# Attention of one block of queries for both kv heads at once, on the two halves of the array; the sums of squares of the mixer's outputs added on DVE

## The chip, the cores and the metric

The kernel runs on one NeuronCore of a Trainium2 chip, as one program. The metric is the device time of one execution in microseconds (us). Five engines run their own instruction streams and wait for each other through semaphores: TensorE (PE, the 128x128 matmul array, with its weight loads shown as PEld), VectorE (DVE), ScalarE (ACT), GpSimd (POOL) and SyncE (SP), which issues the DMAs.

## The reference, cut to what matters

One layer of a hybrid decoder is computed for 1024 prompt positions and 32 sample positions: a half-step FFN, a mixer, a second half-step FFN and a final norm. In the mixer one projection gives q, k, v, u and g. Half of the mixer's output is sliding-window attention, the other half a gated product (gMLP); each half is normalised by itself before the output projection.

```python
def _sink_attention(q, k, v, dist, valid, sinks):
    s = einsum('...qhgd,...khd->...hgqk', q, k) / sqrt(HEAD_DIM)
    s = s - slopes[:, :, None, None] * dist
    s = where(valid, s, -inf)
    p = softmax(concatenate([s, sink], axis=-1), axis=-1)[..., :-1]
    return einsum('...hgqk,...khd->...qhgd', p, v)

def _merge(attn, gate, attn_out_norm, gmlp_out_norm, w_out):
    return concatenate([rmsnorm(attn, attn_out_norm), rmsnorm(gate, gmlp_out_norm)], -1) @ w_out
```

There are 2 kv heads of 64 channels, and 4 query heads go with each (8 query heads in all). The 1024 prompt positions form 8 blocks of 128 queries; a block sees its own 128 keys and the 128 before it (the first block only its own).

## The kernel before

Activations lie with channels on the 128 partitions and tokens along the free axis. Tokens are cut into two halves `h` of 528 (512 of the prompt and 16 of the samples). q, k and v are kept in f32: `QT[h]` has four tiles g of 128 partitions, kv head 0 on partitions 0-63 and kv head 1 on 64-127; `KT` holds the keys in the same way, and `VT` the values with keys on the partitions and the two heads' channels side by side in 128 columns.

The mixer is a list of jobs. For each half come 14 projections (k, v, q0-3, u0-3, g0-3; PSUM tiles `pp`) and then, behind those of both halves, the output projections (`pw`; first the gate's four jobs, then attention's four, for each half). A unit of a projection is 24 matmuls (three for each of eight slices of the contraction, since every f32 operand is split into a high and a low part), a unit of an output projection 12. The weights of a job are loaded into one of six `raw` buffers, cast to a high part on ACT (`whi`, line 114), and the rest is subtracted on DVE or POOL (`wlo`, line 115).

Everything else in the mixer is written as generators that are run in between. The class `Interleave` keeps a clock of PE time, and after each unit it lets as many pieces run as a rate and a credit allow. A piece yields two numbers: the PE time that it cost, and how long its results take, from the table `LAT`; its next piece is run once the clock has passed that. Of the pending generators at most `I.width` run at a time: 1 in the first half's projections, 2 afterwards. After these rules Tile, the layer below, still moves instructions by its own priorities, sets the waits, and gives out buffers. [...]

`attention(b, c)` (lines 844 to 890) treats block b for kv head c, four query heads at a time. First piece: scores `sc` (line 862), two heads to a PSUM bank, on the 64 partitions of head c; a DVE instruction (line 866) that adds the position bias and takes the maximum; `nm`, the negated maximum (867); exp on ACT with the sum (869); the sink's share (870 to 873); and P times the reciprocal (875). Second piece: P is transposed on PE (`ptr`, 881) and copied to `PT` by ACT (882). Third piece: P V into `po` (886), with all 128 columns of `VT` as weights, so that both heads' channels come out, of which ACT copies the 64 partitions of head c over q (888). `count(h, 0, 9)` counts eight such generators and the samples' attention of a half; with the ninth, `norm_out` is put in the queue.

`norm_out(h, which)` takes the squares of the outputs on ACT and adds them (`squares`, line 176, into `oacc`), on POOL unless another engine is given; PE then sums over partitions (`pn`, 150), DVE takes the reciprocal root in some twelve small instructions (`tiny_rsqrt`, 136 to 141), and PE spreads it (`pr`, 165). `spatial` (the gate) transposes g on PE into a PSUM bank `pt` (788), normalises it into `gn` (816, 819) and multiplies it by the spatial weights (`pm`, 835; `mix`, 839). `out_proj` evaluates a unit on DVE (`wo`, 981) and adds it to x on POOL (983). There are eight PSUM banks in the mixer's pool; every `pst` takes one.

Of the kernel before, what the change touches and what calls it, by code (L numbers as in the profile page):

```python
# [11 lines left out]
F32 = mybir.dt.float32  # L12
# [3 lines left out]
AF = mybir.ActivationFunctionType  # L16
ALU = mybir.AluOpType
# [15 lines left out]
RATE = [0.5, 0.67, 0.7, 0.5]  # L33
ON_POOL = {0: (), 1: (), 2: (1, 4, 6)}
STEPS = [(1, 5, 0, 2), (1, 0, 1, 1), (1, 1, 1, 1)]
LAT = {"rstd": 9.0, "gate": 14.7, "qk": 8.5, "pt": 2.5, "gelu": 7.2, "squares": 7.6, "sample": 12, "burst": 6.5, "keys": 9.6, "norm": 6.5, "factors": 10}
GELU_A = 0.044715 ** 0.5
GELU_C = 0.7978845608028654

# [1 line left out]
def build(nc, tc, ctx, A):  # L41
    dbl = ctx.enter_context(tc.tile_pool(name="dbl", bufs=30))
    gp = ctx.enter_context(tc.tile_pool(name="g", bufs=4))
    wp = ctx.enter_context(tc.tile_pool(name="w", bufs=8))
# [13 lines left out]
    V, S, G, PE = nc.vector, nc.scalar, nc.gpsimd, nc.tensor  # L58
# [6 lines left out]
    def gtile(nm, shape=(128, 2, H)):  # L65
        return gp.tile(list(shape), F32, tag="g", name=nm)
# [4 lines left out]
    def pst(nm):  # L71
        return ps.tile([128, 512], F32, tag="ps", name=nm)
# [9 lines left out]
    def small(nm, n=4, p=128):  # L82
        return sp.tile([p, n], F32, tag=f"s_{nm}", name=nm, bufs=1 if nm[0] == "s" else 2 if nm[0] == "g" else 3)
# [13 lines left out]
    ident = cp.tile([128, 128], F32, name="ident")  # L97
# [622 lines left out]
    I = Interleave()  # L720
    finished, have_v = {}, set()

    def count(h, which, of):

        finished[h, which] = finished.get((h, which), 0) + 1
        if finished[h, which] == of:
            finished[h, which] = True
            I.later(norm_out(h, which), wait=LAT["norm"])

# [111 lines left out]
        V.scalar_tensor_tensor(u, m[:, :n], 0.5, u, op0=ALU.mult, op1=ALU.mult)  # L841


    def attention(b, c):
        h, o = b // 4, 128 * (b % 4)
        assert h in have_v
        nk = 256 if b else 128
        rows = slice(64 * c, 64 * c + 64)
        ks = T0[h] + o - 128 if b else 0
        keys = KT[rows, ks:ks + nk]  # L850
        if b == 4:
            keys = KT[rows, 384:672].rearrange("p (a k) -> p a k", a=2)[:, :, :128]
        Pt = gtile("P", (128, 4, 256))
        mx, nm, sm = small("mx"), small("nm"), small("den")
        for j in range(2):
            s = pst("sc")
            for i in range(2):
                g = 2 * j + i
                out = s[:, i * 256:i * 256 + nk]
                if b == 4:  # L860
                    out = out.rearrange("p (a k) -> p a k", a=2)
                PE.matmul(out, lhsT=QT[h](g, o, 128)[rows], rhs=keys, start=True, stop=True)
            for i in range(2):
                g = 2 * j + i
                hd = 4 * c + g
                V.tensor_tensor_reduce(Pt[:, g, :nk], s[:, i * 256:i * 256 + nk], alibi[:, hd, 256 - nk:], 1.0, sinks[:, hd:hd + 1], ALU.add, ALU.max, mx[:, g:g + 1])  # L866
        V.tensor_scalar_mul(nm, mx, -1.0)
        for g in range(4):
            S.activation(Pt[:, g, :nk], Pt[:, g, :nk], AF.Exp, bias=nm[:, g:g + 1], accum_out=sm[:, g:g + 1])
        V.tensor_add(mx, nm, sinks[:, 4 * c:4 * c + 4])  # L870
        S.activation(mx, mx, AF.Exp)
        V.tensor_add(sm, sm, mx)
        V.reciprocal(sm, sm)
        for g in range(4):
            V.tensor_scalar_mul(Pt[:, g, :nk], Pt[:, g, :nk], sm[:, g:g + 1])
        yield 1.8, LAT["qk"]
        PT = gtile("PT", (128, 2, 512))
        for kc in range(nk // 128):
            pt = pst("ptr")
            for g in range(4):  # L880
                PE.transpose(pt[:, g * 128:(g + 1) * 128], Pt[:, g, kc * 128:(kc + 1) * 128], ident)
            S.copy(PT[:, kc, :], pt)
        yield 0.9, LAT["pt"]
        po = pst("po")
        for kc in range(nk // 128):
            PE.matmul(po, lhsT=VT[:, max(b - 1, 0) + kc, :], rhs=PT[:, kc, :], start=(kc == 0), stop=(kc == nk // 128 - 1))  # L886
        for t in range(2):
            S.copy(QT[h].t[t][rows, :, o:o + 128], po[rows, t * 256:(t + 1) * 256].rearrange("p (g q) -> p g q", g=2))
        count(h, 0, 9)
        yield 1.7, 1  # L890


    def sample_attention(h):
        ck = tmp("ck")[:, :512].rearrange("p (b k) -> p b k", b=4)
        load(ck, A["ckT"][:, 4 * h:4 * h + 4, :])
        bc = tmp("bc")[:, :144]
        load(bc, A["sb"])
        bd = tmp("bd")[:, :128].rearrange("p (b r) -> p b r", b=4)
        G.memset(bd, 0.0)
        for c in range(2):  # L900
            rows = slice(64 * c, 64 * c + 64)
            for g in range(4):
                G.tensor_copy(bd[rows, :, 16 * c + 4 * g:16 * c + 4 * g + 4], QT[h](g, 512, 16)[rows].rearrange("p (b t) -> p b t", b=4))
        yield 0.0, 8
        s = pst("ssc")
        for i in range(4):
            r = slice(32 * i, 32 * i + 32)
            PE.matmul(s[r, :128], lhsT=bd[:, i, :], rhs=ck[:, i, :], start=True, stop=True, tile_position=(0, r.start))
        PE.matmul(s[:, 128:144], lhsT=bd.rearrange("p b r -> p (b r)"), rhs=KT[:, T0[h] + 512:T0[h] + 528], start=True, stop=True)
        Sx = tmp("Sx")[:, :144]  # L910
        V.tensor_add(Sx, s[:, :144], bc)
        mc, es, sm = (small(x, 1) for x in ("smc", "ses", "ssm"))
        V.tensor_reduce(mc, Sx, axis=AX.X, op=ALU.max)
        V.tensor_scalar(mc, mc, sinks_s, -1.0, op0=ALU.max, op1=ALU.mult)
        S.activation(Sx, Sx, AF.Exp, bias=mc, accum_out=sm)
        S.activation(es, mc, AF.Exp, bias=sinks_s)
        V.tensor_add(es, es, sm)
        V.reciprocal(es, es)
        V.tensor_scalar_mul(Sx, Sx, es)
        cv = tmp("cv")[:, :512].rearrange("p (b k) -> p b k", b=4)  # L920
        load(cv, A["cvK"][:, 4 * h:4 * h + 4, :])
        yield 1.5, LAT["sample"]
        p1 = pst("sp1")
        PE.transpose(p1[:, :128], Sx[:, :128], ident)
        PE.transpose(p1[:16, 128:256], Sx[:, 128:144], ident)
        t1 = tmp("spt")
        S.copy(t1[:, :128], p1[:, :128])
        S.copy(t1[:16, 128:256], p1[:16, 128:256])
        yield 0.2, 3
        po = pst("spo")  # L930
        PE.matmul(po[:, :128], lhsT=VS[:, h, :], rhs=t1[:16, 128:256], start=True, stop=False)
        for b in range(4):
            c = slice(b * 32, (b + 1) * 32)
            PE.matmul(po[:, c], lhsT=cv[:, b, :], rhs=t1[:, c], start=False, stop=(b == 3))
        pv = po[:, :128].rearrange("p (b c g t) -> p c g b t", b=4, c=2, g=4)
        for c in range(2):
            rows = slice(64 * c, 64 * c + 64)
            for g in range(4):
                V.tensor_copy(QT[h](g, 512, 16)[rows].rearrange("p (b t) -> p b t", b=4), pv[rows, c, g])
        count(h, 0, 9)  # L940
        yield 0.8, 2


# [6 lines left out]
    def norm_out(h, which):  # L950
        src, _ = raw_out(h, which)
        n = T[h]
        acc, r = tmp("oacc"), tmp("orst")
        orst[h][which] = r
        for k in range(4):
            squares(acc, src(k, 0, n), 0, n, k == 0)
        yield 0.0, LAT["squares"]
        yield from rstd(acc, 0, n, 1.0 / 512, 1e-6, lambda p, o: S.copy(r[:, o:o + p.shape[-1]], p))
        done.add((h, which))
# [73 lines left out]
    for job, ahead in zip(jobs, jobs[1:] + [None]):  # L1033
        if job != jobs[0]:
            wnext = weight(*ahead) if ahead else None
        t, h, kind, i = job
        if job == jobs[2]:
            mixer_consts()
        I.width = 1 if t == "p" and h == 0 else 2
        if t == "p":  # L1040
            proj(Pm, h, kind, i, w, RATE[h])
            if (kind, i) == ("q", 3):
                I.later(sample_attention(h))
                for b in range(4 * h, 4 * h + 4):
                    for c in range(2):
                        I.later(attention(b, c))
        else:
            if parts[h][kind] is None:
                split_out(h, kind)
            out_proj(h, kind, i, w, final, RATE[2 + h])  # L1050
            if i == 1 and (h, kind) in ((0, 1), (0, 0)):
                split_out(h if kind else 1, 1 - kind)
        if (t, h, kind, i) == ("o", 0, 0, 3):
            I.later(P2.factors(0), wait=LAT["factors"])
        w = wnext
# [144 lines left out]
```

## Time and profile before

| | us |
|---|---|
| median of 3 runs (lowest to highest) | 1806.27 (1805.62 to 1806.62) |
| the profiled execution | 1804.15 |
| its span, from the first to the last of the program's instructions | 1802.4 |

The profile is of one execution. Rows of the timeline give the start in us from the span's start, the duration of one instruction or of several alike in a row (x8), the engine, the line, and what is written and read. An f32 matmul of the program stands as two passes in the trace (each with a weight load of its own); one of fp32r operands as one. The end of a matmul is modelled, and matmuls overlap in the pipeline, so the distance between starts tells the pace. In lists of waits a row names who waited for whom. The mixer takes the stretch from about 690 to 1095 us: projections of the first half up to about 830, of the second up to 948, output projections to 1095; attention runs from 786 to 1051.

### The profile page before, as it was taken

The numbers are of one execution on the slowest core, as the hardware profiler recorded it, in microseconds if no ns is written. First come the engines' busy times: TensorE is split into PE (matmuls) and PEld (weight loads), VectorE is DVE, ScalarE is ACT, GpSimd is POOL, SyncE is SP. The second block draws the span as 40 slices with busy tenths as digits, with TensorE's granted clock in tenths as the row PEclk, the third lists the DMA queues.
The fourth block names the chain that finished last, engine by engine and source line by source line (L and its number), as shares of the span: only waits on it lengthen the run. The fifth ranks groups of instructions, "written<-read, shape, count | busy, mean of one in ns | idle before, by whom it ended". The sixth has DMA issues, their size and how long they took to land. (4 is left out here: it accounts for less than half of the span.)

```text
span 1802.4 us, 34123 instructions
## 1 busy us (share of the span) xinstructions
PE 1765.7 (98%) x14045; PEld 1729.8 (96%) x14045; DVE 1217.4 (68%) x2171; ACT 740.3 (41%) x1312; POOL 168.6 (9%) x152
## 2 busy tenths in 40 slices
PE   9999999999999999999989999999999999999997
PEld 9999999999999999998878899999999999999997
DVE  7986766676557565486677885986666676457566
ACT  6543333333343453354554644633333333343441
POOL 0000000000000012212212562000000000000110
PEclk9999999999999999999989999999999999999998
DMA  6154544454595344322120222154544454595532
GB/s 237 33 193 160 205 148 149 156 201 140 186 345 179 131 155 144 96 71 64 55 65 28 93 83 95 41 193 157 201 148 154 154 201 137 187 343 188 181 108 97
DMA packets 104460, 266.05 MB, mean 148 GB/s; under 512 B 12384, under 2 KB 15136, under 8 KB 104288
## 3 DMA queue, kind: packets, MB, share of 16 engines
q1 hardware_dynamic: 104304, 263.87, 42.6%
q8 instruction: 110, 1.80, 0.4%
q14 instruction: 46, 0.38, 0.1%
HBM read 190.25 MB, written 74.60 MB: 147 GB/s over the span
## 5 line engine op out<-in xcount | busy, mean ns | idle before, releaser
L430 PE MATMUL pa<-th,wb 128*128 128x264 f32 x2624 | 493.7, 284 | 1.2 <-DVE wb L122 0.6
L430 PEld LDWEIGHTS pa<-th,wb 128*128 128x128 f32 x2624 | 412.3, 188 | 2.6 <-DVE wb L122 0.9
L430 PE MATMUL pa<-tl,wb 128*128 128x264 f32 x1312 | 373.6, 285 | 2.5 <-DVE tl L299 2.5
L620 PE MATMUL pd<-hh,whi 128*128 128x264 f32 x1208 | 343.6, 285 | 0.0
L620 PE MATMUL pd<-hh,wlo 128*128 128x264 f32 x1208 | 343.6, 284 | 0.0
L620 PE MATMUL pd<-hl,whi 128*128 128x264 f32 x1208 | 343.2, 284 | 0.0
L121 ACT CAST wb<-raw 128x512 fp32r<-128x512 f32 x296 | 181.3, 620 | 284.3 <-PE pc L430 82.1
L122 DVE TENSOR_TENSOR wb<-raw,wb 128x512 fp32r<-128x512 f32 x296 | 201.6, 690 | 105.4 <-ACT wb L121 104.8
L430 PEld LDWEIGHTS pa<-tl,wb 128*128 128x128 f32 x1312 | 246.6, 188 | 2.8 <-DVE tl L299 2.7
L430 PE MATMUL pc<-th,wb 128*128 128x264 f32 x1280 | 247.0, 285 | 1.4 <-DVE x L468 0.8
L620 PEld LDWEIGHTS pd<-hh,wlo 128*128 128x128 f32 x1208 | 227.4, 188 | 0.0
L620 PEld LDWEIGHTS pd<-hh,whi 128*128 128x128 f32 x1208 | 227.2, 188 | 0.1
L620 PEld LDWEIGHTS pd<-hl,whi 128*128 128x128 f32 x1208 | 227.2, 188 | 0.0
L430 PEld LDWEIGHTS pc<-th,wb 128*128 128x128 f32 x1280 | 203.3, 188 | 2.0 <-DVE x L468 1.0
L367 DVE TENSOR_TENSOR wlo<-raw,whi 128x1024 fp32r<-128x1024 f32 x82 | 94.7, 1155 | 135.3 <-ACT whi L366 122.5
L430 PE MATMUL pc<-tl,wb 128*128 128x264 f32 x640 | 181.9, 284 | 0.0
L269 DVE TENSOR_TENSOR raw<-raw 128x512 f32<-128x512 f32 x248 | 168.9, 688 | 17.3 <-DMA raw<-f_d 12.3
L366 ACT CAST whi<-raw 128x1024 fp32r<-128x1024 f32 x82 | 79.9, 980 | 217.1 <-PE pd L620 147.0
L130 PE MATMUL pp<-xh,whi 128*128 128x264 f32 x448 | 132.9, 297 | 0.4 <-DVE mx L866 0.4
L130 PE MATMUL pp<-xh,wlo 128*128 128x264 f32 x448 | 128.5, 287 | 0.0
L130 PE MATMUL pp<-xl,whi 128*128 128x264 f32 x448 | 128.2, 286 | 0.0
L430 PEld LDWEIGHTS pc<-tl,wb 128*128 128x128 f32 x640 | 120.3, 188 | 0.3 <-DVE tl L299 0.3
(233 smaller groups left out, 3080.6 us busy)
## 6 DMA issues: line engine op xcount, KB each, us to landing
raw<-f_gu SPq DMA_DIRECT2D x86, 512.0 KB, 4.2
raw<-f_d SPq DMA_DIRECT2D x74, 512.0 KB, 4.0
ws_s<-raw SPq DMA_DIRECT2D x88, 256.0 KB, 2.0
ht<-ht_s SPq DMA_DIRECT2D x40, 528.0 KB, 7.8
raw<-ws_s SPq DMA_DIRECT2D x40, 512.0 KB, 9.0
raw<-w_in SPq DMA_DIRECT2D x28, 512.0 KB, 3.6
ht_s<-m SPq DMA_DIRECT2D x44, 264.0 KB, 2.3
ht<-ht SPq DMA_DIRECT2D x20, 528.0 KB, 3.7
```

The costliest lines, as they stand in the source:

```text
L121: S.copy(w[:, 0], src)
L122: V.tensor_sub(w[:, 1], src, w[:, 0].bitcast(F32))
L130: PE.matmul(p[:, :n], lhsT=w[a][:, c:c + 128], rhs=b(k, o, n), start=(3 * i + j == 0), stop=(3 * i + j == last))
L269: V.tensor_add(b[dst], b[dst], b[x])
L366: S.copy(wh[:, :n * 512], raw[:, :n * 512])
L367: V.tensor_sub(wl[:, :n * 512], raw[:, :n * 512], wh[:, :n * 512].bitcast(F32))
L430: PE.matmul(ps_[:, j], lhsT=w[:, a, kk * 128:(kk + 1) * 128], rhs=b[kk // 2][c][:, kk % 2, j * PC:(j + 1) * PC], start=(start and kk == 0 ...
L620: PE.matmul(ps_[d][:, j], lhsT=w[:, k * 512 + d * 128:k * 512 + (d + 1) * 128], rhs=t[:, k, j * PC:(j + 1) * PC], start=(bi == 0 and oi == ...
```

## The change

One generator `attention(b)` treats both kv heads of a block. The scores of the two heads stand in turn, on rows 0-63 and rows 64-127 of the array, each into its own PSUM bank. P V is computed for each head with its own 64 columns of `VT`, at columns 0-63 and 64-127 of the array, into the two halves of the partitions of one bank `po`, which ACT then copies for both heads at once. The small instructions of softmax (nm, sink, sum, reciprocal) are done for eight heads at once. P moves from a buffer of the pool `g` to two buffers of the pool `raw`, which the weights use as well. `LAT["qk"]` goes from 8.5 to 12.5 and `LAT["pt"]` from 2.5 to 5.0, the costs that the pieces yield from 1.8, 0.9, 1.7 for one head to 1.8, 1.8, 1.8 for both, and the width is 2 everywhere. In `norm_out` the squares of the outputs are added on DVE.

```diff
-LAT = {"rstd": 9.0, "gate": 14.7, "qk": 8.5, "pt": 2.5, ...}
+LAT = {"rstd": 9.0, "gate": 14.7, "qk": 12.5, "pt": 5.0, ...}
...
-    def attention(b, c):
+    def attention(b):
...
-        Pt = gtile("P", (128, 4, 256))
-        mx, nm, sm = small("mx"), small("nm"), small("den")
+        Pt = [wp.tile([128, 4, 256], F32, tag="raw", name="P", bufs=6) for c in range(2)]
+        mx, nm, sm = small("mx", 8), small("nm", 8), small("den", 8)
         for j in range(2):
-            s = pst("sc")
+            s = [pst("sc") for c in range(2)]
             for i in range(2):
-                g = 2 * j + i
-                out = s[:, i * 256:i * 256 + nk]
-                PE.matmul(out, lhsT=QT[h](g, o, 128)[rows], rhs=keys, start=True, stop=True)
+                for c, rows in enumerate(both):
+                    keys, out = KT[rows, ks:ks + nk], s[c][:, i * 256:i * 256 + nk]
+                    PE.matmul(out, lhsT=QT[h](2 * j + i, o, 128)[rows], rhs=keys, start=True, stop=True)
...
-        yield 1.8, LAT["qk"]
-        PT = gtile("PT", (128, 2, 512))
+        yield 1.8, LAT["qk"]
+        PT = [gtile("PT", (128, 2, 512)) for c in range(2)]
...
-        yield 0.9, LAT["pt"]
+        yield 1.8, LAT["pt"]
         po = pst("po")
         for kc in range(nk // 128):
-            PE.matmul(po, lhsT=VT[:, max(b - 1, 0) + kc, :], rhs=PT[:, kc, :], ...)
+            for c, rows in enumerate(both):
+                PE.matmul(po[rows], lhsT=VT[:, max(b - 1, 0) + kc, rows], rhs=PT[c][:, kc, :], ..., tile_position=(0, rows.start))
         for t in range(2):
-            S.copy(QT[h].t[t][rows, :, o:o + 128], po[rows, t * 256:(t + 1) * 256]...)
-        count(h, 0, 9)
-        yield 1.7, 1
+            S.copy(QT[h].t[t][:, :, o:o + 128], po[:, t * 256:(t + 1) * 256]...)
+        count(h, 0, 5)
+        yield 1.8, 1
...
-            squares(acc, src(k, 0, n), 0, n, k == 0)
+            squares(acc, src(k, 0, n), 0, n, k == 0, V)
...
-        I.width = 1 if t == "p" and h == 0 else 2
...
-                    for c in range(2):
-                        I.later(attention(b, c))
+                    I.later(attention(b))
```

The order of PE's instructions changes with it. In the second half's projections, behind a P V, the scores of one kv head of a block stood so before (`po` is P V, `sc` the scores):

```order
L130 MATMUL pp<-xh_7522,wlo 128x264
L886 MATMUL po<-PT,VT 128x512 x2
L862 MATMUL sc<-KT,q_8129 128x256 x2
L862 MATMUL sc<-KT,q_8130 128x256 x2
L130 MATMUL pp<-xh_7519,whi 128x264
```

Now, at such a place near the end of the second half's projections:

```order
L130 MATMUL pp<-xh_7522,wlo 128x264
L889 MATMUL po<-PT,VT 64x512 x4
L860 MATMUL sc<-KT,q_9571 128x256 x4
L860 MATMUL sc<-KT,q_9572 128x256 x4
L130 MATMUL pp<-xh_7519,whi 128x264
```

Four matmuls of P V with 64 output partitions stand where two with 128 stood, and eight of scores where four stood; there are half as many such groups.

The second place is the norm of the first half's attention. Before, PE's sums over `oacc` stood right behind a transposition of P, and ahead of the last gate's transposition and the samples' P V:

```order
L881 MATMUL ptr<-ident,P 128x128 x8
L150 MATMUL pn<-ones,oacc 128x1 x4
L150 MATMUL pn<-ones,oacc 16x1
L788 MATMUL pt<-ident,pv 128x128 x4
L789 MATMUL pt_10636<-ident,pv 16x128
L931 MATMUL spo<-spt,VS 128x128
L934 MATMUL spo<-spt,cv 128x32 x4
```

Now the additions for both norms of the first half stand on DVE among the second half's q (`q_9571` and `q_9572` are its tiles), some 120 projection matmuls ahead of the first `pn`:

```order
L841 SCALAR_TENSOR_TENSOR u_8411<-mix,u_8411 128x16
L176 TENSOR_TENSOR oacc<-oacc,sq 128x528 x2
L759 SCALAR_TENSOR_TENSOR q_9571<-pp,rst 128x264
L176 TENSOR_TENSOR oacc<-oacc,sq 128x528 x4
L759 SCALAR_TENSOR_TENSOR q_9572<-pp,rst 128x264
L115 TENSOR_TENSOR wlo<-raw,whi 128x1024
```

The norms moved from u and g of the second half to its q, and their additions from POOL to DVE.

The third place is DVE where the output projection begins. `gn` and `gns` free the PSUM banks of a gate's transposition. Before, four instructions of a head group's P stood among the reciprocal root for that gate:

```order
L136 TENSOR_SCALAR gt<-gss 128x5
L873 RECIPROCAL den<-den 128x4
L137 TENSOR_SCALAR gr<-gt 128x5
L875 TENSOR_SCALAR P<-P,den 128x256
L139 TENSOR_TENSOR gt<-gr 128x5
L875 TENSOR_SCALAR P<-P,den 128x256
L140 SCALAR_TENSOR_TENSOR gt<-gt,gss 128x5
```

Now eight of them, and three subtractions of weights, stand between the score reductions and that gate's root:

```order
L841 SCALAR_TENSOR_TENSOR u_9930<-mix,u_9930 128x512
L876 TENSOR_SCALAR P<-P,den 128x256 x8
L740 SCALAR_TENSOR_TENSOR pv<-gs,pv 128x264
L839 SCALAR_TENSOR_TENSOR mix<-pm,gains,bss 128x16
L115 TENSOR_TENSOR wlo<-raw,whi 128x1024
L841 SCALAR_TENSOR_TENSOR u_9930<-mix,u_9930 128x16
L115 TENSOR_TENSOR wlo<-raw,whi 128x1024
L816 TENSOR_SCALAR gss<-gss 128x5
```

The last block's softmax, which was still to come, now stands ahead of the gate.

More of the change, by code (lines that the diff above doesn't have):

```diff
@@ L35 @@
 STEPS = [(1, 5, 0, 2), (1, 0, 1, 1), (1, 1, 1, 1)]
-LAT = {"rstd": 9.0, "gate": 14.7, "qk": 8.5, "pt": 2.5, "gelu": 7.2, "squares": 7.6, "sample": 12, "burst": 6.5, "keys": 9.6, "norm": 6.5, "factors": 10}
+LAT = {"rstd": 9.0, "gate": 14.7, "qk": 12.5, "pt": 5.0, "gelu": 7.2, "squares": 7.6, "sample": 12, "burst": 6.5, "keys": 9.6, "norm": 6.5, "factors": 10}
 GELU_A = 0.044715 ** 0.5
@@ L847, in attention @@
         nk = 256 if b else 128
-        rows = slice(64 * c, 64 * c + 64)
+        both = [slice(64 * c, 64 * c + 64) for c in range(2)]
         ks = T0[h] + o - 128 if b else 0
-        keys = KT[rows, ks:ks + nk]
-        if b == 4:
-            keys = KT[rows, 384:672].rearrange("p (a k) -> p a k", a=2)[:, :, :128]
-        Pt = gtile("P", (128, 4, 256))
-        mx, nm, sm = small("mx"), small("nm"), small("den")
+        Pt = [wp.tile([128, 4, 256], F32, tag="raw", name="P", bufs=6) for c in range(2)]
@@ L855, in attention @@
+        mx, nm, sm = small("mx", 8), small("nm", 8), small("den", 8)
         for j in range(2):
-            s = pst("sc")
+            s = [pst("sc") for c in range(2)]
             for i in range(2):
-                g = 2 * j + i
-                out = s[:, i * 256:i * 256 + nk]
[L860 to L866, printed above, removed]
+                for c, rows in enumerate(both):
+                    keys, out = KT[rows, ks:ks + nk], s[c][:, i * 256:i * 256 + nk]
+                    if b == 4:
+                        keys = KT[rows, 384:672].rearrange("p (a k) -> p a k", a=2)[:, :, :128]
+                        out = out.rearrange("p (a k) -> p a k", a=2)
+                    PE.matmul(out, lhsT=QT[h](2 * j + i, o, 128)[rows], rhs=keys, start=True, stop=True)
+            for c in range(2):
+                for i in range(2):
+                    g = 2 * j + i
+                    hd = 4 * c + g
+                    V.tensor_tensor_reduce(Pt[c][:, g, :nk], s[c][:, i * 256:i * 256 + nk], alibi[:, hd, 256 - nk:], 1.0, sinks[:, hd:hd + 1], ALU.add, ALU.max, mx[:, hd:hd + 1])
@@ L867, in attention @@
         V.tensor_scalar_mul(nm, mx, -1.0)
-        for g in range(4):
-            S.activation(Pt[:, g, :nk], Pt[:, g, :nk], AF.Exp, bias=nm[:, g:g + 1], accum_out=sm[:, g:g + 1])
-        V.tensor_add(mx, nm, sinks[:, 4 * c:4 * c + 4])
+        for hd in range(8):
+            x = Pt[hd // 4][:, hd % 4, :nk]
+            S.activation(x, x, AF.Exp, bias=nm[:, hd:hd + 1], accum_out=sm[:, hd:hd + 1])
+        V.tensor_add(mx, nm, sinks)
         S.activation(mx, mx, AF.Exp)
@@ L873, in attention @@
         V.reciprocal(sm, sm)
-        for g in range(4):
-            V.tensor_scalar_mul(Pt[:, g, :nk], Pt[:, g, :nk], sm[:, g:g + 1])
+        for hd in range(8):
+            x = Pt[hd // 4][:, hd % 4, :nk]
+            V.tensor_scalar_mul(x, x, sm[:, hd:hd + 1])
         yield 1.8, LAT["qk"]
-        PT = gtile("PT", (128, 2, 512))
+        PT = [gtile("PT", (128, 2, 512)) for c in range(2)]
         for kc in range(nk // 128):
[L879 to L882, printed above, removed]
-        yield 0.9, LAT["pt"]
+            for c in range(2):
+                pt = pst("ptr")
+                for g in range(4):
+                    PE.transpose(pt[:, g * 128:(g + 1) * 128], Pt[c][:, g, kc * 128:(kc + 1) * 128], ident)
+                S.copy(PT[c][:, kc, :], pt)
+        yield 1.8, LAT["pt"]
         po = pst("po")
         for kc in range(nk // 128):
-            PE.matmul(po, lhsT=VT[:, max(b - 1, 0) + kc, :], rhs=PT[:, kc, :], start=(kc == 0), stop=(kc == nk // 128 - 1))
+            for c, rows in enumerate(both):
+                PE.matmul(po[rows], lhsT=VT[:, max(b - 1, 0) + kc, rows], rhs=PT[c][:, kc, :], start=(kc == 0), stop=(kc == nk // 128 - 1), tile_position=(0, rows.start))
         for t in range(2):
-            S.copy(QT[h].t[t][rows, :, o:o + 128], po[rows, t * 256:(t + 1) * 256].rearrange("p (g q) -> p g q", g=2))
-        count(h, 0, 9)
-        yield 1.7, 1
+            S.copy(QT[h].t[t][:, :, o:o + 128], po[:, t * 256:(t + 1) * 256].rearrange("p (g q) -> p g q", g=2))
+        count(h, 0, 5)
+        yield 1.8, 1
     def sample_attention(h):
@@ L939, in sample_attention @@
                 V.tensor_copy(QT[h](g, 512, 16)[rows].rearrange("p (b t) -> p b t", b=4), pv[rows, c, g])
-        count(h, 0, 9)
+        count(h, 0, 5)
         yield 0.8, 2
```

## The prediction

> **What bounds the kernel now.** I read the page first, then the list of waits on TensorE, then stretches of the span, then the timeline at single groups.
>
> ```profile
> span 1802.4 us, 34123 instructions
> PE 1765.7 (98%) x14045; PEld 1729.8 (96%) x14045; DVE 1217.4 (68%) x2171; ACT 740.3 (41%) x1312; POOL 168.6 (9%) x152
> ```
>
> TensorE (PE) is busy for 98% of the span, so time is won where PE instructions become fewer or shorter, or where one of PE's few waits goes. Every line of the change lies in the mixer, from about 780 to 1095 us. The waits of PE there (columns: who waited for whom, us in total, times, longest):
>
> ```profile
> PE pr L165 <- DVE gv L141: 4.5, 3, 2.6
> PE pn L150 <- POOL oacc L176: 4.1, 1, 4.1
> PE po L886 <- ACT PT L882: 3.7, 2, 2.8
> PE pw L130 <- DVE gn L819: 3.5, 1, 3.5
> ...
> PE pg L396 <- DVE wo L981: 2.4, 1, 2.4
> ```
>
> A wait costs more than its length, because TensorE's granted clock falls behind it. In these stretches the columns are busy time of PE, weight loads, DVE, ACT, POOL, then the granted clock:
>
> ```profile
> 780.00:1095.00 315.00, 301.36 (x2114) 271.00 (x2113) 238.60 (x728) 161.36 (x442) 105.51 (x94) 0.97 0.21 69
> 928.00:940.00 12.00, 11.19 (x50) 10.52 (x51) 5.94 (x26) 4.66 (x17) 0.76 (x1) 0.50 0.08 32
> 944.00:956.00 12.00, 8.06 (x50) 6.57 (x49) 10.87 (x62) 6.64 (x32) 0.00 (x0) 1.00 0.09 37
> 956.00:961.00 5.00, 5.00 (x27) 4.74 (x28) 4.32 (x13) 0.00 (x0) 1.44 (x2) 0.66 0.00 0
> 1021.00:1026.00 5.00, 3.64 (x8) 1.86 (x9) 5.00 (x10) 2.90 (x6) 2.57 (x2) 0.66 0.36 108
> 1100.00:1104.00 4.00, 4.00 (x22) 4.00 (x22) 3.25 (x6) 1.27 (x2) 1.32 (x3) 0.57 0.61 166
> ```
>
> PE idles 315.0 - 301.4 = 13.6 us of the mixer. Behind the 4.1 us wait for POOL the clock is 0.50 over 928 to 940; PE works there from 928.8, so 0.5 x 11.2 = 5.6 us more are lost and the wait costs 9.7 us. Likewise the wait for gn costs 3.5 + 0.34 x 5 = 5.2, the longer of the two waits for PT 2.8 + about 1.5 = 4.3, and the wait for wo 2.4 + 0.43 x 4 = 4.1 us. The next engine is DVE with 238.6 of 315 us (76%), but 10.87 of 12 us from 944 to 956, where PE waited for it.
>
> **The products on the array's halves.** The counts, and groups in the timeline (start, us from first start to last end, instruction, count). Each f32 matmul of the program stands as two passes in the trace.
>
> ```profile
> L862 PE MATMUL sc<-KT,q x128: 272/376/480, 786.3 to 1034.0; 64*128 64x256 f32 x112, 64*128 64x128 f32 x16
> L886 PE MATMUL po<-PT,VT x60: 590/592/1222, 803.3 to 1050.0; 128*128 128x512 f32 x60
> ```
> ```profile
> 786.35 1.16 PE L862 MATMUL sc<-KT,q 64*128 64x128 f32 x8
> 787.43 0.39 PE L130 MATMUL pp<-xh,whi 128*128 128x264 f32 x1
> ...
> 803.34 1.13 PE L886 MATMUL po<-PT,VT 128*128 128x512 f32 x2
> ...
> 906.69 1.98 PE L886 MATMUL po<-PT,VT 128*128 128x512 f32 x4 [0.91 <-ACT PT L882]
> 908.11 0.69 PE L130 MATMUL pp<-xh,whi 128*128 128x264 f32 x1
> ...
> 911.18 0.28 PE L130 MATMUL pp<-xl,whi 128*128 128x264 f32 x1
> 911.30 0.28 PE L130 MATMUL pp<-xh,wlo 128*128 128x264 f32 x1
> 911.51 1.99 PE L862 MATMUL sc<-KT,q 64*128 64x256 f32 x8
> 913.43 0.66 PE L788 MATMUL pt<-ident,pv 128*128 128x128 f32 x4
> ```
>
> *Scores.* One head group of a block is eight passes and takes 913.43 - 911.51 = 1.92 us; the first block, with half the keys, 1.08. It begins 0.21 us behind the last pp where pp follows pp by 0.12, so entering costs 0.09 more, and I take as much for leaving: 2.1 us a group, 1.26 for the first. Before there are two groups a block, on rows 0-63 and on rows 64-127. After, the sixteen passes stand together and alternate between the halves. If the halves run beside each other, the pair takes the time of one group, and one group a block goes: 7 x 2.1 + 1.26 = **16.0 us**.
>
> *P V.* Two more passes cost 1.98 - 1.13 = 0.85 us, so one takes 0.43 and the four of a head group 1.7 us; 60 passes are 25.8. After, each pass fills 64 columns, and two run beside each other: 12.9 us go. But these groups now change the array's shape, which they did not: behind the old one pp started with no gap to speak of, while a score group pays for entering and leaving. Of its 2.1 us, eight passes alone would be 8 x 0.21 = 1.7 (doubling the keys adds 1.99 - 1.16 = 0.83 us to eight passes of 128 columns, so 256 are 0.21 a pass); 0.4 us is the price of both changes. Eight groups: 3.2 us. Net 12.9 - 3.2 = **9.7 us**.
>
> [...]
>
> Whether halves run beside each other has one witness:
>
> ```profile
> 901.06 1.04 PE L881 MATMUL ptr<-ident,P 128*128 128x128 f32 x8
> 902.03 0.43 PE L908 MATMUL ssc<-ck,bd 128*32 128x128 f32 x8
> 902.38 0.40 PE L909 MATMUL ssc<-KT,bd 128*128 128x16 f32 x2
> ```
>
> Eight passes of 128 columns through the whole array take 902.03 - 901.06 = 0.97 us; eight through 32-column strips, four strips in turn, 902.38 - 902.03 = 0.35 us with the change of shape in it. Strips of columns do overlap. Halves of rows stand nowhere next to each other without a wait, so for the scores the gain lies between nothing but the saved changes of shape (8 x 0.4 = 3.2 us) and 16.0; I take 16.0, since the strips are the nearest row.
>
> **The squares on DVE.**
>
> ```profile
> 923.83 4.92 POOL L176 TENSOR_TENSOR oacc<-oacc,sq 128x528 f32<-128x528 f32 x3 [15.63 <-ACT sq L172]
> L176 DVE TENSOR_TENSOR acc<-acc,sq 128x528 f32<-128x528 f32 x4 | 3.4, 841 | 0.0
> ```
>
> PE waited until 928.8 for three adds that POOL took 4.92 us for; on DVE three take 3 x 0.84 = 2.5 us. There are 12 of them, 10.1 us more for DVE. In the new order the two norms of the first half have five units of 24 pp (24 x 0.12 = 2.9 us each) between the last P V and the first pn, so both the adds and the ACT squares ahead of them have 14 us. The 9.7 us go. What is late next there: pr, which waits for DVE's short chain as it did (in the 4.5 us), and stays.
>
> **Fewer small instructions.**
>
> ```profile
> L867 DVE TENSOR_SCALAR nm<-mx 128x4 f32<-128x4 f32 x16 | 4.9, 305 | 0.2
> L870 DVE TENSOR_TENSOR mx<-nm,sinks 128x4 f32<-128x4 f32 x16 | 4.2, 260 | 0.2
> L888 ACT COPY q<-po 64x256 f32<-64x256 f32 x32 | 10.2, 366 | 13.9 <-PE po L886 13.8
> ```
>
> These two kinds on DVE, and two more like them, come once a block: half of 9.1 and about 3 us more, some 7 us, nearly pay for the adds. ACT loses 16 copies of 0.37 (5.9 us). Neither engine ends the mixer; I count nothing.
>
> **The new timing.** Blocks now go in twos through softmax and the transposes, with 12.5 and 5.0 in the table of latencies for 8.5 and 2.5. That moves P V further behind the copies to PT: the two waits for PT (0.9 and 4.3 with its clock, 5.2 us) should go. In exchange eight heads' work arrives on DVE at once. The place to look is where out_proj begins; there DVE was the one waited for:
>
> ```profile
> 944.67 0.48 DVE L866 CUSTOM_DVE_ANT_0 P<-sc,alibi,sinks 128x256 f32<-128x256 f32 x1 [0.32 <-PE sc L862]
> ...
> 952.45 0.34 DVE L875 TENSOR_SCALAR P<-P,den 128x256 f32<-128x256 f32 x1
> ...
> 954.73 1.12 DVE L819 TENSOR_SCALAR gn<-pt,gss 128x128 f32<-128x128 f32 x4
> 955.76 0.33 DVE L819 TENSOR_SCALAR gns<-pt,gss 16x128 f32<-16x128 f32 x1
> L115 DVE TENSOR_TENSOR wlo<-raw,whi 128x1024 fp32r<-128x1024 f32 x26 | 34.4, 1324 | 11.0 <-ACT whi L114 10.9
> ```
>
> From the first score reduction to gn, which frees the PSUM bank that pw wants, DVE took 956.1 - 944.7 = 11.4 us. In the new order the same stretch holds three more P by den (1.0 us), three wlo (3 x 1.2 to 1.3), two al, a mix and a u, and three of gelu's: about 9 us more. PE has about 5 us more between them (24 pp, a gate pair, 12 pw). So the wait grows from 3.5 by 9 - 5 to about 7, less an overlap of neighbouring instructions that the durations count twice: 6, with 2 for the clock, 8 in place of 5.2: **2.8 us worse**; between nothing worse and 8 worse. For a second block's P that is not ready when PE transposes it I put 1.5 (between 0 and 5).
>
> **The sum.** Against the profiled execution, 1804.2 us (1802.4 of them span): 1804.2 - 16.0 - 9.7 - 9.7 (POOL's wait) - 5.2 (PT) + 2.8 + 1.5 = 1767.9. The median of the runs shown is 1806.27, 2.1 above: **1770 us**. FFN2, from 1095 on, has 2.4 us of wait at its head and none until the end's norm, so what the mixer saves reaches the end.
>
> **Rivals.**
> 1. *Passes in strict turn.* If a half's second pass must start before the other half's first, the two overlap only crosswise, and each group lasts one pass longer: 8 x 0.21 + 8 x 0.43 = 5 us, 1775. Against it: the strips' eight passes took the time of three at most. [...]
> 2. *DVE becomes the bound.* 238.6 us plus 3 in a mixer of some 280: 86%, and in bursts. If each of the four pairs costs a wait of 2.5 us, +10: 1780.
> 3. *Row halves don't overlap* (both write all 128 PSUM partitions): 12.8 us of the scores' 16.0 stay away, 1783. If neither kind overlaps, the change does not do what it says: another 12.9, 1796, with the waits alone won.
> 4. *Slower: weights starve.* P moves into the six raw buffers through which weights are loaded; two blocks hold four of them for some 15 us. A late weight costs its load (3.6), cast (1.0) and POOL's subtraction (2.4): 7 us a block, 8 x 7 = 56, against 36 saved: 1826. It decides once a load comes later than it is needed, and for that the lead has to vanish. It is long:
>
> ```profile
> 851.59 0.34 SPq L105 DMA_DIRECT2D raw<-w_in  x1
> raw<-w_in SPq DMA_DIRECT2D x28, 512.0 KB, 3.6
> 904.74 1.03 ACT L114 CAST whi<-raw 128x1024 fp32r<-128x1024 f32 x1
> ```
>
> The last load of w_in is issued at 851.59 and the last cast of one begins at 904.74: 53 us ahead. A third of it, for two buffers left of six, is still 18.
>
> **How the numbers follow.** Forecast (1762 to 1773) 0.50; rival 1 0.13; rival 2 0.16; row halves not overlapping 0.09; nothing overlapping 0.04; starving 0.03; better than the forecast, DVE's burst hidden and the end's wait gone too, 0.05. The range of 1758 to 1787 takes in the first four and leaves out about 0.1 to 0.15. Faster by over 0.2% (about what a measurement of this kernel can tell from no change) holds in all but starving and a little of the nothing-overlaps case with worse waits: 0.95; within 0.02; slower 0.03.
>
> **What would show it.** sc: a group of sixteen passes lasting about 1.9 to 2.0 us; eight of P V in about 1.9 us, pairs starting within a few ns of each other. No wait of pn for oacc, and the clock at 1.0 where it was 0.50. A wait of pw for gn at the head of out_proj of 4 to 8 us. Wrong if the passes of one group start one after another, if PE's waits in the mixer add up to over 20 us, or if casts of weights wait for DMAs.

## The result, and the profile after

The changed kernel takes 1786.0 us (median of 4 runs, 1785.3 to 1787.5) where the kernel before takes 1806.1 beside it: a ratio of 0.989 (95% interval 0.9875 to 0.9905), 20 us faster. Forecast were 1770 us and 36 us of gain, with a range up to 1787. The direction and the range held, the range by 1 us; 16 us of the expected gain are missing.

First the page of the kernel after, for comparison with the same two lines of before:

```profile
span 1783.5 us, 34092 instructions
PE 1741.6 (98%) x14045; PEld 1713.3 (96%) x14045; DVE 1221.6 (68%) x2151; ACT 730.9 (41%) x1288; POOL 158.4 (9%) x140
```

PE is busy for the same share, with as many instructions, so the page alone doesn't tell where the gain went. The mixer does: the stretch from the first projection to the last output projection, of before and then of after (columns as in the prediction: length, busy time of PE, weight loads, DVE, ACT, POOL, granted clock).

```profile
703.60:1095.20 391.60, 377.40 (x2739) 346.06 (x2738) 280.35 (x816) 188.45 (x492) 136.96 (x119) 0.97 0.23 74
```
```profile
704.80:1078.70 373.90, 353.37 (x2740) 329.80 (x2738) 282.88 (x795) 178.14 (x467) 127.00 (x108) 0.97 0.24 77
```

The mixer is 17.7 us shorter. PE's busy time fell by 24.0 us, but its idle time rose, from 14.2 to 20.5. Busy time holds the loss of clock too. In before that was 5.6 + 1.7 + 1.5 = 8.8 us; in after there are four stretches at half clock:

```profile
913.20:920.03 6.83, 6.03 (x27) 6.03 (x28) 6.80 (x16) 1.49 (x5) 3.12 (x2) 0.50 0.50 155
957.60:961.01 3.41, 2.94 (x12) 2.70 (x12) 1.69 (x5) 0.00 (x0) 0.00 (x0) 0.51 0.25 48
964.40:971.23 6.83, 4.69 (x21) 4.64 (x22) 4.92 (x18) 0.75 (x5) 2.90 (x4) 0.50 0.11 43
1022.40:1029.23 6.83, 4.94 (x21) 4.71 (x22) 5.05 (x11) 2.07 (x3) 5.63 (x5) 0.50 0.51 155
```

Half of PE's busy time in them, 0.5 x (6.03 + 2.94 + 4.69 + 4.94) = 9.3 us, is loss (there pw follows pw by 0.22 us in place of 0.12). What PE had to do at full clock therefore went from 377.4 - 8.8 = 368.6 to 353.4 - 9.3 = 344.1: **24.5 us less work, against 25.7 forecast**. Idle and clock together went from 23.0 to 29.8, where the forecast had them fall by 10.6. That is 17 us more than forecast, and with the 1.2 us of the products it is the 18.6 us by which the mixer's gain fell short (36.3 forecast, 17.7 measured). The waits of PE in the mixer after:

```profile
PE pw L130 <- DVE gn L819: 5.5, 1, 5.5
PE pr L165 <- DVE gv L141: 4.7, 2, 4.1
PE pp L130 <- POOL wlo L115: 4.0, 2, 2.1
PE pw L130 <- DVE mix L839: 3.7, 1, 3.7
PE pg L396 <- DVE wo L984: 1.6, 1, 1.6
PE ptr L883 <- DVE gn L819: 1.0, 1, 1.0
```

The waits of pn for POOL's oacc and of P V (`po`) for PT are gone, as forecast. In their place stand three others: weights that come late (wlo), the head of out_proj (gn and mix, 9.1 us), and pr.

**Where each of them comes from.** The late weight first; rows of the timeline of after, by engine:

```profile
909.71 0.49 ACT L869 ACTIVATE P<-P,nm 128x256 f32<-128x256 f32 x1
910.20 0.19 ACT L871 ACTIVATE mx<-mx 128x8 f32<-128x8 f32 x1
910.30 1.03 ACT L114 CAST whi<-raw 128x1024 fp32r<-128x1024 f32 x1
...
911.46 4.86 POOL L115 TENSOR_TENSOR wlo<-raw,whi 128x1024 fp32r<-128x1024 f32 x2 [24.48 <-ACT whi L114]
...
914.00 0.59 PE L130 MATMUL pp<-xh,wlo 128*128 128x264 f32 x1 [2.11 <-POOL wlo L115]
```

ACT had been at the eight exps of a block since 906.25. The cast of the next weight stands behind the last of them, POOL's subtraction behind the cast, and PE runs dry for 2.11 us and then has half clock. Its load (row of SP's queue; the first of the three) had been issued 23 us earlier, so this isn't the starving of rival 4: the weight stood in ACT's queue.

```profile
887.01 27.29 SPq L105 DMA_DIRECT2D raw<-w_in  x3
```

The lead of the projections' loads, from issue to cast, did shrink while attention runs, now that P takes `raw` buffers: it was 37 to 58 us before and is 5 to 29, in places below the 18 I had reckoned with. The closest weight landed 1.1 us before its cast (797.8 and 798.9 us). No cast of the mixer waited for its load.

DVE in the same place, beside the same work where POOL was idle:

```profile
911.39 6.40 DVE L876 TENSOR_SCALAR P<-P,den 128x256 f32<-128x256 f32 x8
```
```profile
955.35 2.18 DVE L876 TENSOR_SCALAR P<-P,den 128x256 f32<-128x256 f32 x8
```

Eight P by den take 2.18 us alone and 6.40 beside POOL's two subtractions. Then the head of out_proj (ACT, DVE and PE in turn):

```profile
955.71 1.03 ACT L114 CAST whi<-raw 128x1024 fp32r<-128x1024 f32 x1
...
957.04 0.28 ACT L814 ACTIVATE junk<-pt 128x128 f32<-128x128 f32 x1
...
961.12 1.04 ACT L114 CAST whi<-raw 128x1024 fp32r<-128x1024 f32 x1 [3.71 <-PE pw L130]
962.07 0.27 ACT L814 ACTIVATE junk<-pt 128x128 f32<-128x128 f32 x1
```
```profile
960.95 1.23 DVE L115 TENSOR_TENSOR wlo<-raw,whi 128x1024 fp32r<-128x1024 f32 x1 [1.72 <-issue]
962.85 0.17 DVE L816 TENSOR_SCALAR gss<-gss 128x5 f32<-128x5 f32 x1 [0.67 <-ACT junk L814]
...
965.27 1.12 DVE L819 TENSOR_SCALAR gn<-pt,gss 128x128 f32<-128x128 f32 x4
```
```profile
958.07 0.59 PE L130 MATMUL pw<-ah,whi 128*128 128x264 f32 x1 [3.67 <-DVE mix L839]
...
966.54 0.56 PE L130 MATMUL pw<-ah,whi 128*128 128x264 f32 x1 [5.46 <-DVE gn L819]
```

The gate's five squares (`junk`) are cut in two by a cast that waits 3.71 us for PE to give back a weight buffer. PE gives it back at the end of its unit at 961 and then waits itself for gn, which needs the last two squares, a chain of twelve small DVE instructions, and the four gn. So ACT and PE hold each other up in turn: the squares stand behind the waiting cast, and PE waits for the squares.

Last pr, where PE waits for the end of a chain of small DVE instructions (`gt`, `gr`, `gv`). One of them, which takes 0.17 us in the chain at 963, beside an addition on POOL, and PE's row:

```profile
1022.40 1.30 POOL L176 TENSOR_TENSOR acc<-acc,sq 128x528 f32<-128x528 f32 x1 [1.44 <-ACT sq L172]
```
```profile
1022.45 1.28 DVE L140 SCALAR_TENSOR_TENSOR gt<-gt,gv 128x5 f32<-128x5 f32 x1
```
```profile
1024.29 0.98 PE L165 MATMUL pr<-ident,gv 128*128 128x128 f32 x3 [4.13 <-DVE gv L141]
```

### The profile page after: what moved, and what is told of

Read it like the earlier page. It is cut to its first block, busy times and chain, and to the rows that moved or that the text cites. A ratio compares the mean times of both kernels' runs of the same rounds, so it can differ in the third digit from the quotient of the medians.

```text
span 1783.5 us, 34092 instructions
## 1 busy us (share of the span) xinstructions
PE 1741.6 (98%) x14045; PEld 1713.3 (96%) x14045; DVE 1221.6 (68%) x2151; ACT 730.9 (41%) x1288; POOL 158.4 (9%) x140
## 4 chain that ended last, share of the span: by engine, by line
PE 79%; DVE 11%; issue 6%; POOL 2%; ACT 2%; DMA 0%; POOLq 0%; SPq 0%; DVEq 0%; ACTq 0%
PE pa L430 24%; PE pd L620 22%; PE pc L430 12%; PE pp L130 7%; PE pb L430 6%; PE pg L396 4%; PE pw L130 2%; POOL x L986 2%; DVE tl L299 1%; DVE wb L122 1%; ACT P L869 1%; DVE P L876 1%; DVE P L865 1%; PE po L889 1%; DVE raw L269 1%
```

## The experiments

Each is the kernel after with the edit shown, unless it says otherwise. Ratios are to the kernel before, run beside it. That kernel's median moved from 1806.1 to 1809.3 us from one set of runs to the next, so a difference of 3 us between medians of different sets is a hint and no more; where the intervals of two ratios overlap or touch, it isn't shown.

### The products

**scores_apart.** The passes of one head in a row, then those of the other.

```diff
-            for i in range(2):
-                for c, rows in enumerate(both):
+            for c, rows in enumerate(both):
+                for i in range(2):
```

> The score passes of a bank pair in another order: four on rows 0-63, then four on rows 64-127, instead of in turn; nothing else differs. If the halves run beside each other only when their passes stand in turn, a group of sixteen loses all but the three overlaps at its changes of half: 13 passes x 0.216 + 0.2 = 3.0 us in place of 1.92, 7.5 groups, 8 us more of PE work: 1789 to 1795 (part of it lands in waits that are there already). If the 1.92 us came from something other than the alternation, the group stays at 1.9 and the time at 1786.

Measured: 1788.0 us, 0.9887 (0.9872 to 0.9902), no difference from after. A group's row in after and here:

```profile
869.43 2.00 PE L860 MATMUL sc<-KT,q 64*128 64x256 f32 x16
```
```profile
778.50 2.10 PE L860 MATMUL sc<-KT,q 64*128 64x256 f32 x16
```

The starts of the sixteen passes, in us from the first:

```
after         0.000 0.007 0.320 0.327 0.536 0.543 0.752 0.759 0.968 0.975 1.184 1.191 1.400 1.406 1.615 1.623
scores_apart  0.000 0.013 0.320 0.333 0.536 0.549 0.751 0.765 0.967 0.981 1.183 1.293 1.399 1.509 1.615 1.725
```

The trace doesn't name a pass's half, but passes on one half follow each other by 0.216 us, so two that start 13 ns apart are on different halves. With the program's order four and four they still start in pairs, and the group is only 0.1 us longer: PE starts the first pass of the second half 0.3 us ahead of the first half's second pass, which stands before it in the program. The halves overlap in both orders; my expectation of 3.0 us a group was wrong, and the alternation in the change is worth 0.1 us a group.

**pv_full.** P V on all 128 columns, one bank for each head.

```diff
-        po = pst("po")
-        for kc in range(nk // 128):
-            for c, rows in enumerate(both):
-                PE.matmul(po[rows], lhsT=VT[:, ..., rows], rhs=PT[c][:, kc, :], ..., tile_position=(0, rows.start))
+        for c, rows in enumerate(both):
+            po = pst("po")
+            for kc in range(nk // 128):
+                PE.matmul(po, lhsT=VT[:, ..., :], rhs=PT[c][:, kc, :], ...)
...
```

> P V as before the change: all 128 columns of the values as weights for each head, one bank for each head, the rest as after. If the column halves gain what the sum said (12.9 us less 3.2 for changes of the array's shape), PE work rises by 9.7 us and the time goes to 1792 to 1798. If changes of shape eat the gain, the time stays at 1786.

Measured: 1795.8 us, 0.9933 (0.9918 to 0.9948): 9.8 us slower than after by the medians (8 by the ratios). The group of a block in after, the same here, and this kernel's mixer:

```profile
894.44 1.94 PE L889 MATMUL po<-PT,VT 128*64 128x512 f32 x8
```
```profile
849.68 3.60 PE L889 MATMUL po<-PT,VT 128*128 128x512 f32 x8
```
```profile
705.00:1088.80 383.80, 362.97 (x2737) 336.64 (x2736) 283.03 (x795) 184.17 (x482) 126.00 (x108) 0.97 0.24 75
```

PE is busy 9.6 us longer with as much idle time (20.8). So the halves of P V are worth what the sum said (9.7), changes of shape included. Of the 24.5 us, 14 to 15 are left for the scores (16.0 forecast), by subtraction: scores_apart kept their overlap, and no run takes it away. The rows bear it out, since sixteen passes take 1.93 us to the next pp where eight took 1.92.

### The squares

**pool_squares.** Only the squares back on POOL.

```diff
-            squares(acc, src(k, 0, n), 0, n, k == 0, V)
+            squares(acc, src(k, 0, n), 0, n, k == 0)
```

> The squares of the outputs added on POOL again, the rest as after. If DVE's adds are what took the wait of pn for oacc away, that wait comes back: 4 us and as much again of clock, 1790 to 1796. If the new order alone hides POOL's adds (14 us between the last P V and the first pn), 1784 to 1788; below 1785 if DVE's ten us of adds were part of the wait of pr for gv.

Measured: 1788.8 us, 0.9893 (0.9878 to 0.9908). No wait of pn for oacc appears, so the new order alone hides POOL's adds. Putting them on DVE is worth 3 us by the medians, which the intervals don't show; the waits of pr are 5.8 us here, 4.7 in after.

**before_squares.** The kernel before with the same edit turned round (`V` added to the call).

> The kernel before with one edit: squares of the outputs added on DVE. If POOL's adds are the whole wait of pn for oacc, 4.1 us and 5.6 of clock go: 1796 to 1798. If ACT's squares, which come late, set it, only the difference of the adds goes (4.9 to 2.5 us) with part of the clock: 1800 to 1804.

Measured: 1798.2 us, 0.9945 (0.9931 to 0.9959), 9 us faster than before. But not by the mechanism of the sum:

```profile
930.79 0.37 PE L150 MATMUL pn<-ones,oacc 128*128 128x1 f32 x1 [3.26 <-DVE oacc L176]
```
```profile
929.00:939.30 10.30, 8.51 (x38) 7.83 (x39) 6.91 (x31) 5.31 (x20) 0.00 (x0) 0.50 0.15 52
```

The wait is still 3.26 us, with half clock behind it. ACT's last square ends at 927.6, as PE begins to wait; DVE's three adds, though shorter than POOL's, stand behind the gate's gn and a weight's subtraction and run from 928.3 to 930.7. What went are the wait of pw for gn (3.5 us, 0.4 left) and that of pr. That gate's squares are done on ACT at 945.9 here, ahead of the exps that begin at 949.7; before, they stood among the exps. Why this edit moves them is open. It also shows that the parts of the diff don't add up: this line is worth 9 us in the kernel before and 3 at most in the changed one.

### The timing

**old_lat.** The two latencies of the table as before.

```diff
-"qk": 12.5, "pt": 5.0
+"qk": 8.5, "pt": 2.5
```

> The table's two latencies as before the change (8.5 and 2.5), the rest as after. If the larger values are what took away the waits of po for PT, these come back: two to four waits of 1 to 3 us with clock, 1790 to 1798. If not, and blocks only come closer together, 1782 to 1789.

Measured: 1813.4 us, 1.0026 (1.0015 to 1.0038): slower than before the change, and far outside both expectations. No wait of po for PT came back. Weights came late instead, and other waits grew too (pr 7.1 us, pm for gn 4.9, ptr for a P that is not ready 4.1):

```profile
PE pp L130 <- ACT whi L114: 13.8, 4, 4.4
```
```profile
813.60 0.59 PE L130 MATMUL pp<-xh,whi 128*128 128x264 f32 x1 [4.40 <-ACT whi L114]
804.40:812.50 8.10, 4.80 (x40) 4.59 (x38) 6.35 (x29) 8.07 (x34) 0.00 (x0) 1.00 0.00 0
```

Two blocks' softmax fall together here: ACT is busy for 8.07 of 8.10 us with sixteen exps, and the cast behind them costs PE 4.4 us, where eight exps cost 2.1 in after. So the products' gain is there only with the larger latencies, a line of the diff: without them waits and clock eat all of it. That they work by keeping blocks apart is what these rows show at one place; for the other waits it is not shown. The other parts of the new timing, the costs that the pieces yield and P in the `raw` buffers, were not tried alone.

**width1**, one generator at a time in the first half's projections (the removed line put back), and **width1_all**, the width 1 throughout.

```diff
+        I.width = 1 if t == "p" and h == 0 else 2
```
```diff
-            self.pending, ..., self.width = deque(), [], 0.0, 0.0, 2
+            self.pending, ..., self.width = deque(), [], 0.0, 0.0, 1
```

> At most one generator at a time in the first half's projections, as before the change; the rest as after. If the late weight at 794 us comes from two blocks' softmax back to back on ACT (fifteen exps in a row ahead of the cast), that wait of 1.9 us and that of ptr for gn at 839 go: 1782 to 1785. If attention of the first half is only pushed to where the second half's work is, the time rises: 1788 to 1795.

> One generator at a time throughout the mixer. Theory of bursts: no two blocks' softmax back to back, so the waits for late weights at 794 and 914 us (4.0 us, and 3.4 of clock) go and that for mix at 958 halves: 1776 to 1782. Against it: attention then reaches some 90 pw units further into out_proj, where POOL's adds to x hold up DVE, and new waits of pw for P V's successors come up: 1786 to 1795.

Measured: 1789.1 us, 0.99 (0.9887 to 0.9914), and 1820.3 us, 1.0076 (1.0061 to 1.009). The first moves the waits but doesn't lessen them: those at the head of out_proj are gone, and at 932 a cast behind sixteen exps in a row costs 5.15 us, in place of 2.11 behind eight at 914. (The late weight at 794 in after, 1.9 us, stands behind eight exps too, not fifteen as I expected; here it is gone.) In the second the last blocks come when no unit is left to stand between their pieces:

```profile
PE ptr L883 <- DVE P L876: 17.1, 2, 9.2
```

PE goes straight from a block's scores to its transposes and waits out the whole softmax, twice. That is a mechanism of the slower side that I hadn't priced.

### DVE, ACT and POOL

**wlo_dve.** The projections' low parts all on DVE.

```diff
-lo_on=G if t == "p" and i else None
+lo_on=None
```

> The low parts of the projections' weights subtracted on DVE, none on POOL; the rest as after. Theory 1: the waits of pp for wlo, and part of those at the head of out_proj, come from POOL: its subtraction takes 2.4 us, and DVE instructions that read and write only SBUF stand still beside it (P times 1/den 1.4 us in place of 0.34). Then the time falls by 4 to 10 us: 1776 to 1782. Theory 2: the waits come from the mere amount of work that eight heads bring to DVE and ACT at once; then 1.2 us more for DVE per weight makes it worse: 1788 to 1795.

Measured: 1782.8 us, 0.986 (0.9844 to 0.9877), 3 us better than after (the two intervals just touch): the sign of theory 1, and less than its 4 to 10 us. The longest wait for a weight fell from 2.1 to 1.6 us, though their sum rose from 4.3 to 5.6; what became less is the time at half clock, from 23.9 to 17.0 us:

```profile
PE pp L130 <- DVE wlo L115: 3.2, 2, 1.6
PE pp L130 <- ACT whi L114: 2.4, 3, 1.5
```

The cast behind the exps stays late, which POOL has no part in.

**gate_first.** The output projection's weights asked for one job later, their casts and subtractions issued behind the gate's last square (`behind[0]`) and last gn (`behind[1]`) of those traced so far, for the first three of each half's four gate groups.

```diff
+            with tc.issue_after(behind[0]):
+                S.copy(hi, raw)
+            with tc.issue_after(behind[1]):
+                V.tensor_sub(lo, raw, hi.bitcast(F32))
...
             out_proj(h, kind, i, w, final, RATE[2 + h])
+            wnext = weight(*ahead) if ahead else None
```

> The casts and subtractions of the output projection's weights are issued one job later and, on their engines, behind the gate's squares and gn; the rest as after. Theory 1 (the order on ACT and DVE: at the head of out_proj a cast that waits for PE to free a weight buffer stands in front of two of the gate's five squares, and a subtraction that waits for the same buffer in front of its chain, and PE waits for their result): the wait of pw for gn, 5.5 us and 3.4 of clock, falls below 2; 1778 to 1782. Theory 2 (DVE simply has too much to do there): the wait stays above 4 us or turns up as pw waiting for wlo; 1785 to 1790.

Measured: 1782.8 us, 0.9864 (0.9851 to 0.9878), 3 us better than after (the intervals touch). The wait for mix is gone, that for gn is not, and a new one stands in the projections:

```profile
PE pw L136 <- DVE gn L827: 4.7, 1, 4.7
...
PE ptr L893 <- DVE P L886: 2.1, 1, 2.1
```

Both theories hold a part: of the 9.1 us at the head of out_proj, 4.4 came from the order, and 4.7 stay because the gate's squares stand behind eight exps on ACT and its chain behind eight P by den on DVE.

**x_dve.** The 64 additions to x in out_proj on DVE.

```diff
-                    G.tensor_add(x, x, t[:, :n])
+                    V.tensor_add(x, x, t[:, :n])
```

> The 64 additions to x in out_proj on DVE in place of POOL; the rest as after. In out_proj of the kernel after, DVE stood still for 19.5 us beside POOL; 64 adds of 0.35 us are 22 us. Theory 1 (POOL holds up the short chain before the second pr): the wait of pr for gv, 4.1 us and 3.4 of clock, falls below 1.5: 1778 to 1782. Theory 2 (the amount of work on DVE decides): 1786 to 1792.

Measured: 1781.1 us, 0.9843 (0.9825 to 0.9861), 5 us better than after, as theory 1 had it.

```profile
PE pw L130 <- DVE wo L984: 2.7, 2, 2.3
...
PE pr L165 <- DVE gv L141: 0.5, 1, 0.5
```

The wait of pr fell from 4.1 us to nothing in the mixer's second norm, with its half clock; a wait of 2.3 us for wo came up elsewhere. DVE took on 64 more instructions and PE waited less for it.

**combo** (wlo_dve and gate_first) and **combo_x** (and x_dve).

> Both edits at once: all low parts of the projections' weights on DVE, and the output projection's casts and subtractions behind the gate. If the two waits they take away are independent, 3.2 and 3.3 us add up: 1779 to 1780. If DVE's added work stands in front of the gate's chain, 1782 to 1786.

> These two edits and the additions to x on DVE as well: POOL then does nothing in the mixer that DVE waits for. Theory 1: 1773 to 1777. Theory 2, DVE too full: 1782 to 1790.

Measured: 1780.1 us, 0.9841 (0.9823 to 0.9858), and **1775.2 us, 0.9813 (0.9795 to 0.983)**. By the medians the parts add up: 3.2 + 3.3 + 4.9 = 11.4 us against 10.8. The last is faster than both kernels; its interval lies clear of that of after. Its mixer and its largest waits:

```profile
706.50:1071.70 365.20, 347.87 (x2739) 324.95 (x2739) 285.35 (x873) 179.97 (x471) 24.28 (x32) 0.99 0.25 80
```
```profile
PE pw L136 <- DVE gn L827: 4.9, 1, 4.9
PE pw L136 <- DVE wo L994: 4.0, 3, 1.7
```

POOL's busy time in the mixer fell from 127 to 24 us, and DVE's rose by only 2.5 although it does those 103 us of POOL's work: what it took over it got back in time not spent held up. In after, some 40 DVE instructions of out_proj that overlap with POOL take about 19 us more in sum than the same forms without it, and over the whole mixer the excess is some 48 us.

## Why the prediction was right, and where it was wrong

PE's work was forecast rightly, its waits were not: idle time and loss of clock rose by 6.8 us where they were to fall by 10.6. By the prediction's own sign (waits of PE of over 20 us in the mixer) this part was wrong, with 20.5 us of idle time. That the time lies in the range, by 1 us, is partly luck: the range reached so far for rivals 1 to 3, and none of them is what happened. Rival 2 comes nearest, for the bursts of eight heads did cost waits; but DVE is not the bound, since the kernel with still more work on DVE (combo_x) is faster.

- **The products on the halves: right.** 25.7 us forecast (16.0 + 9.7), 24.5 measured in all; a group of sixteen score passes takes 1.93 us to the next pp, eight of P V 1.87, as written. P V's net 9.7 with its price for changes of shape was measured at 9.6 of PE's busy time and 9.8 of the time (pv_full). Rival 1 is out: pairs start 7 ns apart and each pair takes the time of one pass. Rival 3 is out too, though its 1783 lies nearer to the measured time than the forecast: a time that fits is no evidence for a mechanism.
- **POOL's wait: gone, for half the reason given.** The 9.7 us went, but the new order suffices for that without the adds on DVE (pool_squares), and the adds alone don't do it (before_squares); the 14 us of slack that the text names would have hidden POOL's 4.9 as well.
- **PT's waits: gone, and the latencies did more than that.** They were priced at 5.2 us. With the old latencies the kernel is some 25 us slower by the ratios (old_lat), and not by those waits: two blocks' exps then stand in a row on ACT, ahead of a weight's cast.
- **The head of out_proj: right place, wrong size.** 8 us forecast with clock, 9.1 + 0.5 x (2.94 + 4.69) = 12.9 measured. The sum counted DVE's work alone, the weights' subtractions included, but not that their cast waits for PE inside the gate's own work; with it out of the way (gate_first) the wait without clock falls to 4.7.
- **"For a second block's P that is not ready when PE transposes it I put 1.5": the step that failed most.** P was ready (with the old latencies it is late, by 4.1 us). What was late were weights, behind the exps on ACT: 4.0 us of waits, 1.0 for gn and 3.0 of clock. I had looked for late weights only at the DMAs (rival 4), and not in the queue of the engine that casts them.
- **"pr ... stays": wrong by 5 us.** The waits of pr in the mixer went from 1.9 us to 4.7 and 2.5 of clock. The prediction gave no reason for that beyond how it was before. The chain is twelve instructions that use only SBUF, and some of them take longer beside POOL's additions (1.28 us in place of 0.17 for the one shown above); with those to x on DVE the wait of 4.1 us is gone (x_dve).

From the forecast to the measured change of the mixer: the products 1.2 us short, the head of out_proj 4.9 more than priced, late weights and the wait of ptr for gn 6.5, pr 5.3: together 17.9 of the 18.6 us by which the profiled mixer missed its forecast. Late weights behind the exps are read from the rows, and a longer run of exps costs more (1.9 and 2.1 us behind eight, 4.4 and 5.15 behind sixteen); a run with the cast moved ahead of the exps was not made.

## What to carry to other kernels

Taking work together on PE makes bursts on the engines behind it: ask of each engine's queue what will now stand behind the burst, weight casts and small chains above all, and not only how much work the engine has. A load that arrives early is late all the same if its cast is queued behind the softmax: here one issued 23 us ahead of its cast still cost PE a wait of 2.11 us. Before moving work to an idle engine, look at whether the busy one slows down beside it: here 103 us of POOL's work in the mixer, moved to DVE, raised DVE's busy time by 2.5 us.

## What the hardware showed that was not expected

**In scores_apart, TensorE went past queued passes of one half of the array to start the other's.** A pass of the second half starts 0.013 us after the first, 0.3 us ahead of a pass that stands before it in the program (read from the pace, as above).

**Some DVE instructions that use only SBUF took several times as long beside POOL.** P by den takes 0.34 us alone (0.28 in the first block) and up to 2.47 beside POOL: of the sixteen in the kernel after that meet one of its subtractions, six take 2.41 to 2.47 us and ten 0.28 to 0.35, as alone. One of the smallest instructions takes 2.33 in place of 0.17 when it meets a subtraction:

```profile
794.24 2.33 DVE L870 TENSOR_TENSOR mx<-nm,sinks 128x8 f32<-128x8 f32 x1
```

The reductions of the scores, which read PSUM, took no longer there: the two that lie wholly within a subtraction take 0.48 us, as without one. POOL's subtraction also grew, from 2.40 us to as much as 3.33. What decides which instructions are held up is not shown here.
